# A planner that adds a delay to each result of a recurrent chain, and projections beside it that are given start times

## The chip, the cores and the metric

The kernel runs on one core of a Trainium2 chip. What counts is the device time of one execution in microseconds, here the median of several runs. A core has TensorE (matmul; PE in the profile), VectorE (DVE), ScalarE (ACT), GpSimd (POOL) and SyncE (SP), which here issues most DMAs. Each engine works through its own list of instructions in order and waits for the others by semaphores.

## The reference

Two layers of a backbone over 512 latent and 256 context tokens, width 1024, float32. In each layer a norm, one wide input projection, three token mixers side by side (A: gated linear attention, B: windowed attention, C: RWKV-7 in both directions), a gated merge of their outputs, and a gated feed-forward network. In layer 1 only the latent tokens are needed behind the mixers.

```python
def rwkv7_scan(r, w, k, v, kk, a, s0, with_out):      # mixer C, one direction
    def step(S, inp):
        w_t, k_t, v_t, kk_t, a_t = inp[:5]
        sa = jnp.einsum('bhvk,bhk->bhv', S, kk_t)
        S = S * w_t[:, :, None, :] - sa[..., None] * (kk_t * a_t)[:, :, None, :] + v_t[..., None] * k_t[:, :, None, :]
        ...
        return S, jnp.einsum('bhvk,bhk->bhv', S, inp[5])
    s_fin, y = lax.scan(step, s0, xs)

def merge_branches(ys, gate_logits, w_branch, w_out):
    gates = jnp.split(gate_logits, N_BRANCH, axis=-1)
    m = jax.nn.sigmoid(gates[0]) * (ys[0] @ w_branch[0])
    for i in range(1, N_BRANCH):
        m = m + jax.nn.sigmoid(gates[i]) * (ys[i] @ w_branch[i])
    return m @ w_out
```

## The kernel before

All matrices are cut into tiles of 128 rows. A float32 product is made from three products of a high and a low part (`wh`, `wl`, `hh`, `hl`). A layer runs through the norm, mixers A and B, then the stage that the change touches, then the last branch product, the merge and the feed-forward network.

The touched stage computes mixer C in chunks of 32 tokens. The 768 tokens are six groups of four chunks; a forward and a backward direction (`f`, `b`) go through the groups in opposite orders. Each of these is a stream of operations:

- `loads` and `load_v` bring a group's operands in; `prep` (line 1564) scales them and makes `X`, the products within a chunk.
- `invert` (line 1638) inverts the triangular 32 × 32 blocks of one group of both directions at once. It sends `X` to DRAM (line 1657), reads it back spread out as `L` (line 1660), runs 31 pairs of VectorE instructions (`ftmp`, `G`, lines 1669 and 1670), sends `G` to DRAM (line 1676) and reads it back as the factors `TT` (line 1679). `G` and `L` have one buffer each, so one inversion follows the other.
- `chain` (line 1681) carries the state through the 24 chunks of its direction: `yp` on TensorE, its copy `ysb` on ScalarE, `up` on TensorE with the factors `TT`, copies into `uv` on ScalarE, `sp` on TensorE, and the new state `sblkf` or `sblkb` on VectorE (line 1751). The old state's scaling `scf`, `scb` (line 1719) may run on VectorE, GpSimd or ScalarE.
- `tails` finishes a group's output once both directions have passed it.
- `beside` (line 487) runs work that the chain doesn't need: 24 jobs of 24 products, 16 gate projections and 8 branch products of mixers A and B. In layer 0 each product has a part of 512 and one of 256 columns (`px`, `pz`), in layer 1 only the first. Each job needs its weights loaded (`raw`), split (`wh`, `wl`) and a bank of PSUM; gates leave through ScalarE (line 547), branch products through VectorE (line 576).

The order of all these instructions is made by a planner, `Flow` (line 1866), while the program is built. A stream yields an `Op` with its engine, its cost, what it reads, writes, takes and gives back, and the planner keeps a clock for each engine. It takes the stream whose next operation could start first (its bias is added to that time), books the cost, and notes when the result is there: for TensorE 0.2 us after the end, for a DMA its given latency. A reader on another engine waits 0.12 us more. Only the order of instructions reaches the chip, not the planned times. `chain`, `load_v`, `after` and `summed` (the last two lie in `beside`) have the bias 0, `prep` and `invert` 0.2, the loads of weights 0.2, the products 0.6, the tails 0.4.

Of the kernel before, what the change touches and what calls it, by code (L numbers as in the profile page):

```python
# [19 lines left out]
NX, NZ, NT = 512, 256, 768  # L20
# [8 lines left out]
class Kern:  # L29
    def __init__(self, ctx, tc, I, out, dbg=None):  # L30
        self.ctx, self.tc, self.nc = ctx, tc, tc.nc
        self.I, self.out, self.dbg = I, out, dbg or {}
        self.jobs = deque()
        self.ready = deque()
        self.LOOK = 2
        self.gxb, self.more = 2, None
        self.pin, self.mark = 2, None
        self.hops, self.done = None, 0.0
# [448 lines left out]
    def beside(self, F, l, n, W):  # L487
# [5 lines left out]
        parts = ((0, NX), (NX, n)) if n > NX else ((0, NX),)  # L493
        raws, ws, px, yh, yl, gl = {}, {}, {}, {}, {}, {}
        gw = lambda a, b: 0.232 if b - a == NX else 0.12
        def raw():
            for j, src in enumerate(srcs):
                for e in range(2):
                    yield Op("SP", 0.55, (), ("raw", j, e), take=(("raw", (j, e)),), lat=3.5)
                    raws[j, e] = W.tile([128, 512], F32, name="raw", tag="raw", bufs=3)  # L500
                    nc.sync.dma_start(raws[j, e], src[:, 512 * e:512 * e + 512])
# [22 lines left out]
        def gemms():  # L524
            for j in range(16):
                for a, b in parts:
                    yield Op("PE", 0.0, take=(("gx", (j, 0, a)),))
                    bank(j, 0, a, b)
                for e in range(2):
                    for a, b in parts:  # L530
                        for c in range(4):
                            yield from product(j, 0, a, b, e, c, e == 0, self.h(0, 4 * e + c, a, b), self.h(1, 4 * e + c, a, b))
            yield Op("PE", 0.0, (), "h")
            for j in range(16, 24):
                for o in range(2):
                    for a, b in parts:
                        yield Op("PE", 0.0, (("yab", o),), take=(("gx", (j, o, a)),))
                        bank(j, o, a, b)
                        for c in range(4):
                            yield from product(j, o, a, b, o, c, True, yh[o, c][:, a:b], yl[o, c][:, a:b])  # L540
# [742 lines left out]
class Rwkv:  # L1283
# [354 lines left out]
    def invert(self):  # L1638


        nc, T = self.nc, self.T
        for i in range(6):
            k = lambda name, d="": (name, d, i)
            gs = {d: self.SEQ[d][i] for d in "fb"}
            yield Op("ACT", 0.45, (), k("G"), take=(("G", i),), lat=3.3)
            G = T.tile([128, 2, 8, 32], F32, name="G", tag="G", bufs=1)
            nc.scalar.dma_start(G, self.I["gid"])
            d1, L = {}, None
            for z, d in enumerate("fb"):
# [9 lines left out]
                L = L or T.tile([128, 2, 32, 32], F32, name="L", tag="L", bufs=1)  # L1659
                nc.sync.dma_start(L[:, z].rearrange("u j i -> u (j i)"), d1[d].rearrange("q u j i -> (q u) (j i)").unsqueeze(1).to_broadcast([32, 4, 1024]))  # L1660
            tmp = None
            for n in range(31):
                a, m = n // 4 + 1, 31 - n
                yield Op("DVE", 2 * (0.158 + 0.00105 * 2 * a * m), (k("L", "f"), k("L", "b"), k("G")), k("T"), give=(("L", i),) if n == 30 else ())
                if tmp is None:
                    tmp = T.tile([128, 256], F32, name="ftmp", tag="ftmp", bufs=1)
                t = tmp[:, 0:2 * a * m].rearrange("q (d a b) -> q d a b", d=2, b=m)
                o = G[:, :, 0:a, n + 1:32]
                nc.vector.tensor_tensor(out=t, in0=G[:, :, 0:a, n:n + 1].to_broadcast([128, 2, a, m]), in1=L[:, :, n:n + 1, n + 1:32].to_broadcast([128, 2, a, m]), op=ALU.mult)  # L1669
                nc.vector.tensor_tensor(out=o, in0=o, in1=t, op=ALU.subtract)  # L1670
# [184 lines left out]

class Op:

    def __init__(self, eng, cost=0.0, read=(), write=None, take=(), give=(), lat=None, psum=False):
        self.psum = psum
        self.engs = None if isinstance(eng, str) else eng  # L1860
        if self.engs:
            eng, cost = eng[0]
        self.eng, self.cost, self.read, self.write, self.take, self.give, self.lat = eng, cost, read, write, take, give, lat


class Flow:
# [22 lines left out]

    def begin(self, op):  # L1890

        t = 0.0
        for r in op.read:
            if r not in self.at:
                return None
            at, eng = self.at[r]
            t = max(t, at + (self.HOP if eng != op.eng else 0.0))
        seen = {}
        for tag, _ in op.take:
            bufs, turn, end = self.tags[tag]  # L1900
            i = len(turn) + seen.get(tag, 0) - bufs
            seen[tag] = seen.get(tag, 0) + 1
            if i >= 0:
                if i not in end:
                    return None
                t = max(t, end[i] + self.HOP)
        if op.lat is not None:
            t = max(t, self.dmas[0])
        return t

    def run(self):
        while True:
            heads = []
            for s in list(self.list):
# [12 lines left out]
                if r is not None:  # L1927
                    op = s[2]
                    if op.engs:
                        op.eng, op.cost = min(op.engs, key=lambda e: max(r, self.idle(e[0], op)) + e[1] + self.DEAR.get(e[0], 0.0))  # L1930
                    t = max(r, self.idle(op.eng, op))
# [12 lines left out]
            _, t, s = best  # L1944
# [8 lines left out]
            if op.lat is not None:  # L1953
                self.dmas.append(done)
            if op.write:
                self.at[op.write] = done, op.eng if op.lat is None else "DMA"
            for tag, own in op.take:
                turn = self.tags[tag][1]
# [160 lines left out]
```

## Time and profile before

| what | us |
|---|---|
| median of 3 runs (3235.82 to 3251.81) | 3243.07 |
| the profiled execution | 3247.46 |
| its span, first to last instruction | 3245.6 |
| TensorE busy, share of the span | 2951.2 (91%) |
| VectorE busy | 1760.7 (54%) |
| ScalarE busy | 1202.0 (37%) |
| mixer C's stage, layer 0 | about 650 to 1096 |
| mixer C's stage, layer 1 | about 2345 to 2757 |

The profile holds one execution. Times in it run from the first instruction. A busy TensorE is not one at its peak, since matmuls overlap and their ends are modelled. The granted clock is given as a share of 2.4 GHz: 1.00 is that, 0.50 is 1.2 GHz, and numbers between are means over a stretch.

### The profile page before, as it was taken

What the parts mean: (1) busy time and instruction counts of PE and PEld (TensorE: products, weight loads), DVE (VectorE), ACT (ScalarE), POOL (GpSimd) and SP (SyncE); (2) the same over time, 40 slices, a digit from 0 to 9 for tenths busy, and PEclk for the clock granted to TensorE, in tenths of its full rate; (3) what the DMA queues carried; (4) which work ended last, traced back from release to release, by engine and by line L of the source; (5) the groups of instructions that cost most, each with busy time, mean ns of one, the idle gap of its engine ahead of it and who ended that gap; (6) DMA issues with size and microseconds to landing.
All of it is one profiled execution on the core that took longest, in us unless ns stands there. A gap on an engine that the chain in (4) does not pass through costs nothing. (4 is left out here: it accounts for less than half of the span.)

```text
span 3245.6 us, 62087 instructions
## 1 busy us (share of the span) xinstructions
PE 2951.2 (91%) x25760; PEld 2362.6 (73%) x25760; DVE 1760.7 (54%) x3455; ACT 1202.0 (37%) x2498; POOL 558.7 (17%) x429
## 2 busy tenths in 40 slices
PE   6999999879989889999999899889779887899998
PEld 3777877657767678888888787667556665888887
DVE  3185666766786745222223536646567767653335
ACT  3154454435443333212112434444335444332223
POOL 3033212200001222101001203212200111220102
PEclk9999999889989989999999899989889885899999
DMA  7421322355455542443222322213365652623333
GB/s 292 159 77 59 105 73 106 106 168 157 144 161 163 163 159 91 147 160 134 62 65 79 106 78 82 76 69 104 134 187 162 183 154 62 201 72 98 93 102 117
DMA packets 276282, 398.30 MB, mean 123 GB/s; under 512 B 96928, under 2 KB 178592, under 8 KB 276000
## 3 DMA queue, kind: packets, MB, share of 16 engines
q1 hardware_dynamic: 250528, 360.77, 34.9%
q10 hardware_dynamic: 25472, 33.56, 3.1%
q8 instruction: 202, 3.31, 0.4%
q14 instruction: 80, 0.66, 0.1%
HBM read 320.33 MB, written 73.92 MB: 121 GB/s over the span
## 5 line engine op out<-in xcount | busy, mean ns | idle before, releaser
L50 PE MATMUL px<-hh,wh 128*128 128x512 f32 x1584 | 644.3, 407 | 14.8 <-ACT gat L473 4.6
L50 PE MATMUL px<-hl,wh 128*128 128x512 f32 x1584 | 636.8, 402 | 9.2 <-POOL hl L302 7.9
L50 PE MATMUL px<-hh,wl 128*128 128x512 f32 x1584 | 636.8, 402 | 5.8 <-DVE wl L510 3.1
L71 ACT ACTIVATE wh<-raw 128x1024 fp32r<-128x1024 f32 (+1 forms) x266 | 275.5, 1039 | 722.4 <-PE pz L50 375.6
L72 DVE TENSOR_TENSOR wl<-raw,wh 128x1024 fp32r<-128x1024 f32 (+1 forms) x266 | 333.0, 1253 | 341.5 <-ACT wh L71 311.5
L50 PEld LDWEIGHTS px<-hh,wh 128*128 128x128 f32 x1584 | 304.3, 192 | 105.3 <-issue 25.8
L50 PEld LDWEIGHTS px<-hh,wl 128*128 128x128 f32 x1584 | 304.1, 192 | 81.6 <-issue 8.0
L50 PEld LDWEIGHTS px<-hl,wh 128*128 128x128 f32 x1584 | 304.1, 192 | 77.3 <-POOL hl L302 13.1
L50 PE MATMUL pz<-hh,wl 128*128 128x256 f32 x872 | 250.7, 288 | 1.3 <-DVE wl L72 0.8
L50 PE MATMUL pz<-hh,wh 128*128 128x256 f32 x872 | 249.9, 288 | 2.1 <-DVE fs L729 1.4
L50 PE MATMUL pz<-hl,wh 128*128 128x256 f32 x872 | 250.0, 287 | 1.9 <-DVE hl L304 1.4
L739 POOL TENSOR_TENSOR al<-fs,ah 128x768 fp32r<-128x768 f32 (+1 forms) x44 | 85.0, 1931 | 727.8 <-ACT ah L738 727.8
L50 PE MATMUL px<-y,wh 128*128 128x512 f32 (+1 forms) x512 | 158.8, 395 | 35.1 <-ACT y L123 13.6
L50 PEld LDWEIGHTS pz<-hh,wh 128*128 128x128 f32 x872 | 167.3, 192 | 10.9 <-issue 2.3
L50 PEld LDWEIGHTS pz<-hl,wh 128*128 128x128 f32 x872 | 168.1, 193 | 9.1 <-issue 2.0
L50 PEld LDWEIGHTS pz<-hh,wl 128*128 128x128 f32 x872 | 168.0, 193 | 6.0 <-issue 3.9
L50 PEld LDWEIGHTS px<-y,wh 128*128 128x128 f32 x512 | 96.1, 211 | 58.7 <-ACT y L123 14.3
L1736 ACT COPY uv<-up 32x128 f32<-32x128 f32 x384 | 98.1, 255 | 69.6 <-PE up L1727 57.6
L50 PE MATMUL px<-ah,wh 128*128 128x512 f32 x296 | 116.1, 393 | 0.0
L1670 DVE TENSOR_TENSOR G<-G,ftmp 128x120 f32<-128x120 f32 (+24 forms) x372 | 108.8, 293 | 12.8
L1669 DVE TENSOR_TENSOR ftmp<-G,L 128x120 f32<-128x120 f32 (+24 forms) x372 | 107.3, 288 | 15.4 <-DMA L<-d 5.3
L50 PE MATMUL px<-ah,wl 128*128 128x512 f32 x296 | 115.3, 390 | 0.0
(460 smaller groups left out, 5776.1 us busy)
## 6 DMA issues: line engine op xcount, KB each, us to landing
raw<-w SPq DMA_DIRECT2D x104, 512.0 KB, 3.5
araw<-wada SPq DMA_DIRECT2D x96, 512.0 KB, 5.0
raw<-win SPq DMA_DIRECT2D x82, 512.0 KB, 3.5
raw<-w SPq DMA_DIRECT2D x48, 448.0 KB, 3.4
raw<-win SPq DMA_DIRECT2D x64, 256.0 KB, 3.4
kr<-krd SPq DMA_DIRECT2D x24, 512.0 KB, 4.9
L<-d SPq DMA_DIRECT2D x24, 512.0 KB, 4.5
gs<-gat ACTq DMA_DIRECT2D x24, 384.0 KB, 3.1
```

The source lines that it names most:

```text
L50: return self.nc.tensor.matmul(out, lhsT=lhsT, rhs=rhs, start=start, stop=stop)
L71: nc.scalar.activation(h[:, :n], raw[:, :n], AF.Copy)
L72: nc.vector.tensor_tensor(out=lo[:, :n], in0=raw[:, :n], in1=h[:, :n].bitcast(F32), op=ALU.subtract)
L739: nc.gpsimd.tensor_tensor(out=al, in0=s, in1=ah.bitcast(F32), op=ALU.subtract)
L1669: nc.vector.tensor_tensor(out=t, in0=G[:, :, 0:a, n:n + 1].to_broadcast([128, 2, a, m]), in1=L[:, :, n:n + 1, n + 1:32].to_broadcast([128, ...
L1670: nc.vector.tensor_tensor(out=o, in0=o, in1=t, op=ALU.subtract)
L1736: nc.scalar.copy(uv[ru, p].rearrange("q e v -> q (e v)"), up[32 * p:32 * p + 32, :])
```

## The change

The planner adds 0.6 us to the time at which a result is there, if its stream has the bias 0 and it is not a DMA; buffers that the same operation gives back come free as much later. An operation can be given a time before which the plan doesn't start it (`since`). In layer 1, where a product has one part, job j of `beside` gets 14 j us, and for the branch products the second half 7 us more; in layer 0 nothing is set. The planned cost of a pair of `invert` goes from 2 (0.158 + 0.00105 e) to 2 (0.17 + 0.0012 e), with e elements a row.

```diff
@@ beside
+        pace = 0.0 if n > NX else 14.0
...
-                    yield Op("PE", 0.0, take=(("gx", (j, 0, a)),))
+                    yield Op("PE", 0.0, take=(("gx", (j, 0, a)),), since=pace * j)
...
-                        yield Op("PE", 0.0, (("yab", o),), take=(("gx", (j, o, a)),))
+                        yield Op("PE", 0.0, (("yab", o),), take=(("gx", (j, o, a)),), since=pace * (j + 0.5 * o))
@@ invert
-                yield Op("DVE", 2 * (0.158 + 0.00105 * 2 * a * m), (k("L", "f"), k("L", "b"), k("G")), k("T"), give=(("L", i),) if n == 30 else ())
+                yield Op("DVE", 2 * (0.17 + 0.0012 * 2 * a * m), (k("L", "f"), k("L", "b"), k("G")), k("T"), give=(("L", i),) if n == 30 else ())
@@ Op
-    def __init__(self, eng, cost=0.0, read=(), write=None, take=(), give=(), lat=None, psum=False):
-        self.psum = psum
+    def __init__(self, eng, cost=0.0, read=(), write=None, take=(), give=(), lat=None, psum=False, since=0.0):
+        self.psum, self.since = psum, since
@@ Flow.begin
-        t = 0.0
+        t = op.since
@@ Flow.run
             if op.write:
+                if s[1] == 0.0 and op.eng and op.lat is None:
+                    done += 0.6
                 self.at[op.write] = done, op.eng if op.lat is None else "DMA"
```

## Rows read from the trace of the kernel before

**Rows 1.** Busy time by stretch: start:end, length, engines (instructions), clock, DMA, GB/s

```profile
650.00:1096.00 446.00, 402.17 (x5853) 308.46 (x5852) 319.46 (x777) 190.09 (x545) 42.67 (x34) 0.92 0.52 155
2345.00:2757.00 412.00, 342.20 (x4935) 247.24 (x4930) 292.03 (x719) 178.66 (x513) 44.36 (x35) 0.81 0.51 149
2345.00:2660.00 315.00, 271.10 (x3659) 196.76 (x3654) 230.20 (x544) 142.74 (x387) 35.83 (x28) 0.90 0.59 174
2660.00:2757.00 97.00, 71.10 (x1276) 50.48 (x1276) 61.83 (x175) 35.91 (x126) 8.53 (x7) 0.52 0.27 68
```

**Rows 2.** Same view, instructions of `px` alone: PE, PEld, DVE, ACT, clock, DMA

```profile
2660.00:2685.00 25.00, 0.00 (x0) 0.00 (x0) 0.00 (x0) 0.00 (x0) 0.52 0.49 124
```

**Rows 3.** Costliest groups of the page: count, busy us, mean ns, idle before

```profile
L1670 DVE TENSOR_TENSOR G<-G,ftmp 128x120 f32<-128x120 f32 (+24 forms) x372 | 108.8, 293 | 12.8
L1669 DVE TENSOR_TENSOR ftmp<-G,L 128x120 f32<-128x120 f32 (+24 forms) x372 | 107.3, 288 | 15.4 <-DMA L<-d 5.3
```

**Rows 4.** Stretches of the VectorE phases: layer 1's first, last, sum; layer 0's sum

```profile
2376.90:2401.90 25.00, 10.26 (x93) 8.51 (x92) 23.01 (x72) 4.90 (x9) 1.32 (x1) 0.66 0.31 99
...
2686.70:2708.00 21.30, 12.96 (x224) 9.17 (x224) 18.93 (x70) 7.49 (x28) 0.00 (x0) 0.50 0.06 20
sum 167.90, PE 134.08 PEld 97.12 DVE 147.40 ACT 75.25 POOL 12.49; mean PE 22.35 PEld 16.19 DVE 24.57 ACT 12.54 POOL 2.08
...
sum 200.40, PE 177.88 PEld 136.65 DVE 170.67 ACT 91.52 POOL 20.66; mean PE 29.65 PEld 22.77 DVE 28.45 ACT 15.25 POOL 3.44
```

**Rows 5.** Timeline, VectorE, layer 1: start, length, engine, line, operation

```profile
2401.72 0.19 DVE L1670 TENSOR_TENSOR G<-G,ftmp 128x16 f32<-128x16 f32 x1
```

**Rows 6.** Line 1660 near 2425, the second load of L: issue and landing

```profile
L1660 SPq DMA_DIRECT2D L<-d x1: 519/519/519, 2425.1 to 2425.1; - x1
...
DMA to landing us min/median/max: 5.6/5.6/5.6
```

**Rows 7.** Timeline, VectorE; in brackets the idle time before and its releaser

```profile
2433.39 0.88 DVE L1751 TENSOR_TENSOR sblkb<-sp,scb 64x256 f32<-64x256 f32 x2 [1.20 <-PE sp L50]
2434.30 0.87 DVE L1719 TENSOR_TENSOR scb<-sblkb,pc 64x256 f32<-64x256 f32 x2
2435.20 0.22 DVE L1669 TENSOR_TENSOR ftmp<-G,L 128x62 f32<-128x62 f32 x1
...
2437.59 0.86 DVE L1751 TENSOR_TENSOR sblkf<-sp,scf 64x256 f32<-64x256 f32 x2 [1.40 <-PE sp L50]
```

**Rows 8.** Stretches from L's landing to the next inversion, sums: layer 0, layer 1

```profile
sum 28.00, PE 28.00 PEld 20.52 DVE 15.46 ACT 11.74 POOL 0.25; mean PE 5.60 PEld 4.10 DVE 3.09 ACT 2.35 POOL 0.05
...
sum 21.50, PE 21.50 PEld 14.74 DVE 13.78 ACT 11.63 POOL 4.21; mean PE 4.30 PEld 2.95 DVE 2.76 ACT 2.33 POOL 0.84
```

**Rows 9.** Timeline, VectorE: the longest wait within a phase, layer 0 and layer 1

```profile
828.10 0.86 DVE L1751 TENSOR_TENSOR sblkb<-sp,scb 64x256 f32<-64x256 f32 x2 [4.52 <-PE sp L50]
...
2624.24 0.86 DVE L1751 TENSOR_TENSOR sblkb<-sp,scb 64x256 f32<-64x256 f32 x2 [2.29 <-PE sp L50]
```

**Rows 10.** Timeline, VectorE, layer 1: two successive forward state updates among projections

```profile
2492.65 0.88 DVE L1751 TENSOR_TENSOR sblkf<-sp,scf 64x256 f32<-64x256 f32 x2 [1.46 <-PE sp L50]
...
2500.14 0.86 DVE L1751 TENSOR_TENSOR sblkf<-sp,scf 64x256 f32<-64x256 f32 x2 [1.07 <-PE sp L50]
```

**Rows 11.** Timeline, TensorE, layer 1: two successive `sp`, one of each direction

```profile
2675.22 1.12 PE L50 MATMUL sp<-uv,bkt 64*64 64x64 f32 x16
...
2679.02 1.12 PE L50 MATMUL sp<-uv,bkt 64*64 64x64 f32 x16
```

**Rows 12.** Timeline, VectorE, layer 1's last group: first and fourth backward update

```profile
2729.03 0.88 DVE L1751 TENSOR_TENSOR sblkb<-sp,scb 64x256 f32<-64x256 f32 x2 [1.55 <-PE sp L50]
...
2755.26 0.86 DVE L1751 TENSOR_TENSOR sblkb<-sp,scb 64x256 f32<-64x256 f32 x2
```

**Rows 13.** Timeline, TensorE: the first product behind the stage, layer 0 and layer 1

```profile
1107.88 1.65 PE L50 MATMUL px<-y,wh 128*128 128x512 f32 x3 [6.40 <-ACT y L123]
...
2757.92 0.79 PE L50 MATMUL px<-y,wh 128*128 128x256 f32 x2 [1.98 <-ACT y L123]
```

## The prediction

> **What bounds the kernel now.** I read the two stages first, by the table of stretches [rows 1]. The stage that the change touches takes 446 us in layer 0 and 412 us in layer 1, of a profiled execution of 3247.46 us. TensorE is busy 402 and 342 us of them, so it is not idle long, but in layer 1 the last 97 us are different: the granted clock there is 0.52 (nearly all at the lower level, 1.2 GHz), and the projections are over (no projection matmul in the next 25 us, [rows 2]).
>
> Then I looked for what repeats. Per layer the kernel makes six inversions, one behind the other: 62 VectorE instructions (lines 1669 and 1670), by the page (108.8 + 107.3)/12 = 18.0 us each [rows 3]. In layer 1 the first begins at 2376.9 and the sixth ends at 2708.0 [rows 4], 331 us of the 412. The six VectorE phases add to 167.9 us, so the five intervals between them take 163 us. One such interval, in order of time: the last subtraction of the first inversion starts at 2401.72 [rows 5]; the result goes to DRAM and back, the next block goes out, and the last load of L is issued at 2425.1 and takes 5.6 us, so it lands at 2430.7 [rows 6]. The next inversion starts only at 2435.20. In the 4.5 us between, VectorE executes state updates of the chain which wait for TensorE's `sp` (1.20 us ahead of the one at 2433.39), and the inversion is queued behind them on VectorE [rows 7]. I call this the **hand-over**. All ten add to 28.0 us in layer 0 and 21.5 us in layer 1 [rows 8]. The remaining 163 − 21.5 = 142 us, 28.3 us each, are DMA legs.
>
> So the stage is bounded by a serial loop: DMA legs 28, hand-over 4 to 6, VectorE phase 28 to 33. Inside the phases the same wait occurs again: 12 waits of state updates on `sp` in layer 0, 16.2 us in all, the longest 4.52, and 5 in layer 1, 6.8 us, the longest 2.29 [rows 9]. The chain has slack in each turn of the loop; it ends the stage only after the last inversion.
>
> **The change, part by part.** No instruction is added or removed. All four edits alter the planner's clock, and through it the order on each engine.
>
> Edit 1, +0.6 us on each result of the streams with bias 0. One chain step in the plan (yp, ysb, up, u, sp, S with 0.12 between engines and 0.2 after TensorE) is 0.57 + 0.40 + 0.52 + 1.22 + 0.72 + 1.00 = 4.43 us; with six delays it is 8.03. In a stretch full of projections the trace shows 7.49 us between two updates of one direction [rows 10]. So the plan lags by 3.1 us a step. By the code's latencies the factors TT of the forward direction land 16.8 us before the next L; 16.8/4.43 puts 3.8 steps of the forward chain ahead of the next inversion on VectorE, and, since the backward factors land 5.3 us later, 2.6 of the backward one. Three steps lag 9.3 us; the legs themselves lag 28.8 − 25.4 = 3.4 us behind the plan's; that leaves 5.9 us of waiting, beside a measured mean of 49.5/10 = 4.95. The arithmetic holds, so I use it for after: 16.8/8.03 and 11.5/8.03 put 2.1 and 1.4 steps ahead.
>
> Layer 1: TensorE's own share of two chain steps is 2 × 1.9 us at full clock (3.80 a step near the half clock, [rows 1, 11]). Projections, spread by the pace, fill 5.57/14 = 40% of a slot of 8.03, 3.2 us, and prep and changes of stationary operand about 1; in sum 8.0, no lag. The hand-over falls to between 0 and 1 us. I take −21 of 21.5 and −7 of the waits inside the phases. Against it: about one state update per turn, 0.88 us, with its scaling, 0.87 us [rows 7], moves from the legs, where VectorE has time, into the phase: 5 × 1.75 = +9. Layer 1: −19.
>
> Layer 0: there the projections are half as many again (by the code 576 matmuls of 256 columns more) and unpaced, so the free part of a slot, 8.03 − 2.84 = 5.2 us, is mostly filled: 3.8 + 5.2 + 1 to 2.3 = 10.0 to 11.3 us a step, a lag of 2.0 to 3.3. Two steps lag 4.0 to 6.6 us, less 3.4: a hand-over of 0.6 to 3.2 us instead of 5.6, so −12 to −25; I take −15, near the slower end, since the observed 7.49 was also above its parts. Inside the phases the lag goes on growing over two to three further steps: between −5 and +15; I take +4. The moved update costs +9 again. Layer 0: −2.
>
> Edit 2, the pace in layer 1: job j of 24 not before 14 j us in the plan, the last half at 329. Ahead of that it removes the saturation reckoned above. At the end, projections now run beside the last group. There the chain alone took 8.7 us a step, (2755.26 − 2729.03)/3, at the half clock [rows 12]; at about 8 us: −3, with bounds of −13 (full clock, no projection in the way: the plan's 4.43 and 1 for prep) and +10 (11.3 a step, reckoned above). The weights of the next stage were loaded long before, since the projections' buffers were free by 2660. Now these come free late. Layer 0, where projections run to the end, waits 6.40 us on its first operand behind the stage, layer 1 1.98 [rows 13]; that bounds the cost by 0 and +4.4; I take +2. Edit 3 replaces the plan's cost of one inversion, 16.3 us (sum over line 1664), by 18.0, which is what the page shows [rows 3]; what it does alone is within the bounds above, I put it at 0. Edit 4 (the same +0.6 on gates and branch sums) delays release of a projection bank in the plan; the other bank's twelve or more matmuls cover that, and if not, it is 0.6 us × 24 a layer in the plan only: 0 here, +5 as bound.
>
> A rule to weigh against edit 2: first the rows. With chain work alone TensorE was busy 73% of the last 97 us, and the granted clock was 0.52; in the 315 us before, with projections, it was 0.90 [rows 1]. The Trainium skill (TensorE: Matmul & The Clock Gate, HAM oscillation — how this bites in real kernels) says that bursts of matmuls with idle time between them fall back to the half clock again and again, and that work should be kept together; by that, spreading the projections is the wrong direction. The sum by the rows is the one above; by the rule it is rival 3.
>
> **Sum**: −19 − 2 − 3 + 2 = −22, so 3225.5 us for an execution like the profiled one. That one lies 4.4 us above the median of the three runs (3243.07), so the forecast is 3221, rounded to **3222**.
>
> **Rivals.**
> 1. *The wait only moves.* More projection between two chain steps makes each step longer by as much as the plan now allows, and the updates that no longer hold up the start of an inversion hold up its middle. For it: TensorE is busy 28.00 of the 28.00 us of layer 0's hand-overs [rows 8], so `sp` is late for work, not for order. Against: layer 1 has spare TensorE time over its stage. Then −22 shrinks to about −3: 3240.
> 2. *The whole wait goes.* If layer 0 also loses its hand-overs and phase waits, 13 of its hand-overs and 16 + 4 in its phases are more than I took: 33 us, so 3189 with all of it, 3196 with four fifths. For it: all these waits have the one releaser, `sp` [rows 7, 9].
> 3. *Clock.* In layer 1 TensorE's work per turn at full clock is 8 × 1.9 + 4 × 5.6 + about 8 for prep = 45 us, in a turn of 331/5.5 = 60 us. It becomes the bound when the mean granted clock of the stage falls under 45/60 = 0.75; it is 0.81 now [rows 1]. At 0.69 a turn is 65 us, +5 × 6 = +30, with layer 1's gain gone: 3243 + 30 − 5 = 3268. For it: the 0.52 above. Against: in layer 0 jobs of 5.6 + 2.9 us follow each other about every 446/24 = 19 us, and the clock is 0.92.
> 4. *The stretched last group*, slower. If layer 0's projections still reach into the group after its last inversion, its four steps take 11.3 instead of about 8: +13, and phase waits at their bound another +11, while layer 1 gives −10: 3257. It decides by whether more than two of the 24 jobs are left then.
> 5. *The pace does not spread.* Planned times are not kept on the chip; if the planned stage is shorter than 329 us, the jobs beyond it stand behind the chain, 5.6 us each. With three of them, +17 eats the gain: 3239. My sum of the plan's parts (29 before the first inversion, five turns of 46 to 52, 25 + 10 + 36 at the end) is 330 to 360, so it should just fit.
>
> **How the numbers follow.** Forecast 0.46 (its own range 3208 to 3234), rivals in order 0.14, 0.15, 0.08, 0.10, 0.07. The range 3187 to 3258 leaves out rival 3, half of rival 4 and a third of rival 2, 0.18. A measurement of this kernel can tell about 0.5% from no change, 16 us, so faster is under 3227: 0.37 of the forecast and rival 2, 0.52. Same: the rest of the forecast, rival 1 and most of rival 5, 0.29. Slower, over 3259: rival 3, rival 4 with its edge, and the tail of rival 5, 0.19.
>
> **What would show it.** Right: the ten hand-overs add to 15 to 25 us instead of 49.5; three to four state updates, not six, stand between the factors' landing and the next inversion; projections run past 2700 in layer 1 and the clock of its last 97 us rises above 0.8. Edit 1 wrong: hand-overs shorter and VectorE phases longer by the same. Edit 2 wrong: projections behind the last state update, or the stage's clock under 0.75. The forecast is wrong if layer 1's stage does not shorten by at least 10 us, or if layer 0's grows.

## The result, and the profile after

The changed kernel takes 3275.28 us (median of 5 runs, 3259.58 to 3280.84) beside 3245.69 us for the kernel before on the same chip (5 runs): ratio 1.007, 95% interval 1.0041 to 1.0098 (the two medians alone would give 1.009). The forecast was 3222 us (3187 to 3258), a gain of 0.7%; what came is a loss of 0.7%. The profiled execution, the fastest of the five, took 3259.58 us (span 3257.7), 12.1 us more than that of before.

The table takes the profiled executions apart as the prediction did, in us (L0 and L1 are the layers). A *leg* runs from the last subtraction of an inversion to the landing of the next L, a *hand-over* from there to the next inversion's first instruction, a *phase* over an inversion's VectorE instructions. "Delay" and "pace" are runs of these edits alone, told below. Up to 0.6 us beside the sums of [rows 4] and [rows 8] are where the stretches were cut.

| part | L1 before | L1 after | L1 delay | L1 pace | L0 before | L0 after | L0 delay |
|---|---|---|---|---|---|---|---|
| 5 legs | 141.8 | 139.3 | 135.2 | 142.9 | 133.7 | 166.4 | 153.0 |
| 5 hand-overs | 21.4 | 25.3 | 15.5 | 33.3 | 27.4 | 16.5 | 17.0 |
| 6 phases | 167.9 | 178.1 | 174.4 | 166.8 | 201.0 | 194.5 | 196.5 |
| last phase to the chain's last copy | 47.3 | 45.7 | 46.8 | 46.2 | 53.0 | 47.9 | 52.5 |
| to the first product behind the stage | 2.6 | 2.9 | 2.8 | 2.4 | 10.1 | 3.0 | 3.0 |
| sum | 381.0 | 391.3 | 374.7 | 391.6 | 425.2 | 428.3 | 422.0 |

The 12.1 us are +3.1 and +10.3 in the two stages, 3.9 less ahead of the first, 3.5 less between them, and 6.3 more behind layer 1's stage (494.0 us from its first product to the end, 487.7 before). How far such sums differ by chance can be seen in layer 0: ten profiled executions have the same plan there (before, e2, e5 to e11 and e13), and their sums go from 420.7 to 427.7, their hand-overs from 25.3 to 27.6, their legs from 133.5 to 139.2.

The stages of after by stretch, the same view as [rows 1]: start:end, length, busy us of PE, PEld, DVE, ACT, POOL, then granted clock, DMA share, GB/s.

```profile
650.00:1096.00 446.00, 411.38 (x5782) 316.05 (x5783) 307.55 (x744) 195.46 (x570) 38.14 (x33) 0.90 0.54 156
2345.00:2757.00 412.00, 343.95 (x4832) 246.81 (x4832) 268.81 (x675) 186.26 (x549) 37.77 (x28) 0.80 0.51 148
2345.00:2660.00 315.00, 264.11 (x3548) 191.80 (x3549) 206.41 (x510) 146.06 (x411) 30.52 (x23) 0.81 0.53 153
2660.00:2757.00 97.00, 79.85 (x1285) 55.01 (x1283) 62.40 (x165) 40.20 (x138) 7.26 (x5) 0.77 0.45 128
```

The mean clock of layer 1's stage is what it was, 0.80 beside 0.81. But the last 97 us have risen from 0.52 to 0.77, and the 315 us before have fallen from 0.90 to 0.81. The mean hides that; the intervals between two inversions show it. First before (same view, layer 1), then after:

```profile
2401.91:2435.20 33.29, 28.93 (x420) 19.75 (x418) 19.18 (x35) 15.24 (x46) 1.34 (x1) 0.95 0.66 180
2464.67:2498.59 33.92, 33.92 (x499) 24.18 (x497) 20.31 (x36) 16.94 (x48) 3.88 (x5) 1.00 0.68 185
2525.22:2557.88 32.66, 30.94 (x583) 23.00 (x581) 23.62 (x38) 16.16 (x46) 5.16 (x3) 0.85 0.71 195
2587.54:2621.48 33.94, 32.99 (x515) 23.91 (x514) 21.50 (x33) 15.68 (x46) 10.41 (x8) 0.98 0.64 180
2657.42:2686.74 29.32, 20.84 (x427) 14.40 (x428) 10.74 (x23) 8.15 (x33) 2.31 (x2) 0.56 0.51 136
```

```profile
2398.34:2431.92 33.58, 32.19 (x405) 23.35 (x402) 17.26 (x29) 14.76 (x41) 4.28 (x3) 0.90 0.64 171
2459.01:2489.66 30.65, 23.50 (x349) 17.83 (x347) 16.87 (x25) 12.04 (x34) 2.64 (x3) 0.82 0.67 181
2519.82:2557.32 37.50, 30.55 (x450) 22.45 (x450) 14.43 (x25) 16.38 (x46) 5.06 (x3) 0.77 0.60 160
2584.79:2618.00 33.21, 20.88 (x415) 16.51 (x413) 17.39 (x28) 15.39 (x44) 4.41 (x4) 0.54 0.62 172
2653.33:2682.91 29.58, 27.25 (x294) 19.11 (x293) 13.05 (x22) 10.28 (x30) 1.77 (x1) 0.94 0.79 225
```

Projections lie where the plan was told to put them. In the stretch where before had none [rows 2], `px` alone (PE, PEld, DVE, ACT, clock, DMA) shows in after:

```profile
2660.00:2685.00 25.00, 15.70 (x53) 9.53 (x51) 3.44 (x5) 0.00 (x0) 0.93 0.78 220
```

The first products behind the two stages, as in [rows 13], by the timeline of TensorE:

```profile
1106.98 1.22 PE L50 MATMUL px<-y,wh 128*128 128x512 f32 x2 [4.60 <-ACT y L123]
...
2763.78 0.80 PE L50 MATMUL px<-y,wh 128*128 128x256 f32 x2 [3.23 <-ACT y L123]
```

The sums of the hand-overs (layer 0, layer 1) and of layer 1's phases, as in [rows 8] and [rows 4], then layer 1's sixth phase by itself:

```profile
sum 16.56, PE 16.56 PEld 12.28 DVE 14.23 ACT 8.16 POOL 1.40; mean PE 3.31 PEld 2.46 DVE 2.85 ACT 1.63 POOL 0.28
...
sum 25.28, PE 23.79 PEld 17.06 DVE 14.49 ACT 12.61 POOL 1.85; mean PE 4.76 PEld 3.41 DVE 2.90 ACT 2.52 POOL 0.37
...
sum 178.12, PE 155.51 PEld 106.30 DVE 148.18 ACT 92.83 POOL 10.53; mean PE 25.92 PEld 17.72 DVE 24.70 ACT 15.47 POOL 1.75
...
2682.91:2715.20 32.29, 28.26 (x485) 18.59 (x484) 26.81 (x85) 16.84 (x59) 0.00 (x0) 0.98 0.45 136
```

So the delay did in layer 0's hand-overs what it should (27.4 to 16.5 us), and in layer 1 the hand-overs grew by 4 us and the phases by 10. Of the phases the sixth alone grew by 11, from 21.3 [rows 4] to 32.3 us, of which VectorE was busy 26.8 instead of 18.9: the jobs beside it bring work to VectorE too, the splits of their weights and their sums.

What VectorE didn't work in layer 1's phases and hand-overs, length less busy time, is its waiting: 28.2 us before (20.5 and 7.7), 40.7 after (29.9 and 10.8). Its work there hardly changed (161.2 and 162.7 us), so this waiting is what the loop lost.

### The profile page after: what moved, and what is told of

Its sections match the earlier page's. It is cut to its first block, busy times and chain, and to the rows that moved or that the text cites. A ratio compares the mean times of both kernels' runs of the same rounds, so it can differ in the third digit from the quotient of the medians.

```text
span 3257.7 us, 62093 instructions
## 1 busy us (share of the span) xinstructions
PE 2967.5 (91%) x25760; PEld 2374.0 (73%) x25760; DVE 1735.2 (53%) x3425; ACT 1223.8 (38%) x2578; POOL 544.3 (17%) x419
## 5 line engine op out<-in xcount | busy, mean ns | idle before, releaser
L50 PE MATMUL px<-y,wh 128*128 128x512 f32 (+1 forms) x512 | 157.1, 394 | 32.2 <-ACT y L123 17.0
L50 PEld LDWEIGHTS px<-y,wh 128*128 128x128 f32 x512 | 97.1, 214 | 52.5 <-ACT y L123 17.6
L50 PE MATMUL px<-al,wh 128*128 128x512 f32 x296 | 115.3, 389 | 0.0
```

Of the source, the lines that this page charges most:

```text
L50: return self.nc.tensor.matmul(out, lhsT=lhsT, rhs=rhs, start=start, stop=stop)
```

## The experiments

### Each edit alone

```diff
# e1: delay 0.6, no pace, old cost       # e2: pace 14, no delay, old cost
# e3: new cost of an inversion alone     # e4: after, but buffers come free without the 0.6
```

> The 0.6 us on results alone; the pace and the old cost of an inversion are as before. Theory A (the delay holds back the chain, the chain gives back the operand buffers of layer 0 late, so X of the third and fourth inversion is late): layer 0's legs before the third and fourth inversion stay at 40 us or more (24.4 and 29.0 before), layer 0's loop is about 10 us longer, layer 1 within 5 us of before, the whole +5 to +20 us. Rival B (the loss is all from the pace): within 5 us of the kernel before, legs of layer 0 at 25 to 30 us.

Measured: 3243.82 us, ratio 0.9983 (0.9963 to 1.0004). Hand-overs fell in both layers, by much less than 21 in layer 1. The time is as rival B had it; theory A's legs of 40 us did not come, though two of layer 0 grew to 35.8 and 35.9. VectorE waits 27.0 us in layer 1's phases and hand-overs, nearly what it did before.

> Start times in layer 1 alone, no delay, old cost. Theory A: layer 0 is as before; in layer 1 the projections run beside the last inversion, whose phase grows from 21 to 30 us or more, and the weights of the next stage come late: +8 to +18 us. Rival B: +20 us or more, the whole loss. My prediction would have given -3 to -20.

Measured: 3266.51 us, ratio 1.0063 (1.0041 to 1.0084). The pace alone carries the loss. The sixth phase is 30.9 us, as theory A had it; that the hand-overs would grow, to 33.3 us, neither expected. The sums of layer 1's phases and hand-overs put VectorE's waiting at 25.2 and 17.0, 42.2 us:

```profile
sum 166.83, PE 134.91 PEld 96.01 DVE 141.65 ACT 75.26 POOL 12.77; mean PE 22.48 PEld 16.00 DVE 23.61 ACT 12.54 POOL 2.13
...
sum 33.36, PE 32.79 PEld 22.00 DVE 16.38 ACT 14.53 POOL 0.72; mean PE 6.56 PEld 4.40 DVE 3.28 ACT 2.91 POOL 0.14
```

> The planned cost of an inversion's pairs alone. Theory A and rival B both: within 5 us of before. A third theory, that any change of the plan scatters the time by 10 us and more: off by over 10 us in either direction.

Measured: 3258.54 us, ratio 1.0018 (1.0000 to 1.0037): at the edge of what can be told from nothing. Kernel e7 below, a control, shows the same (1.0019). So a plan that is merely another one can move the time by some 0.2%, and differences of 0.1 to 0.3% say little of a cause; the pace's 0.63% is three times that.

> The changed kernel, but the 0.6 us reach readers only, not the release of buffers that the same operation gives back. Theory A in its narrow form (late planned release by 0.6 us holds the loads back): legs of layer 0 before the third and fourth inversion back to 30 us or less, 10 us faster than the changed kernel. If the chain itself is late (its steps are planned 3.6 us longer), the legs stay at 40 us and the time within 5 us of the changed kernel.

Measured: 3268.19 us, ratio 1.0053 (1.0031 to 1.0076), not to be told from after. Layer 0's legs before the third and fourth inversion are 33.0 and 36.6 us (after 41.3 and 43.7), between the two theories. The later release of buffers in the plan costs nothing that can be measured here. The three edits add up within their intervals: −0.17 + 0.63 + 0.18 = 0.64%, beside 0.70% for all of them.

### Which half of the pace, and what in it

```diff
# e5: gates only                                   # e6: branch products only
-  since=pace * (j + 0.5 * o)                      -  since=pace * j
+  since=0.0                                       +  since=0.0
```

> The kernel before with start times in layer 1 for the 16 gate jobs alone (14 j us); the 8 branch products follow as early as they can, and there is no delay and the old cost. In the run of the pace alone the five hand-overs of layer 1 were 33.3 us instead of 21.4, its first five VectorE phases 135.9 instead of 146.7, and its last turn (fifth leg and sixth phase) 61.1 instead of 46.1. Theory T (the loss of the pace is the last turn, where projections now lie beside the sixth inversion; what the earlier turns lose in hand-overs they win in phases): ratio 0.999 to 1.002, sixth phase 21 to 24 us, hand-overs about 30, earlier phases about 137. Theory H (the loss is in the hand-overs, and the last turn is only where it shows): ratio 1.004 to 1.007, hand-overs 30 or more with the earlier phases not shorter than before.

Measured: 3268.91 us, ratio 1.0058 (1.0040 to 1.0076); hand-overs 38.8 us, sixth phase 34.9.

> The other half: start times for the 8 branch products alone (from 224 us on, 7 us apart in the plan), gates as before. Theory T: this carries the loss of the pace, ratio 1.004 to 1.007, sixth phase 29 to 33 us instead of 21.2, hand-overs of the first four turns as before (17 us), and the last update of the state 10 to 15 us later behind the last softmax product than the 409 us of before. Theory H: ratio 0.999 to 1.002, with the sixth phase longer but the turns before it shorter by as much, since nothing of the branch products lies in them.

Measured: 3259.24 us, ratio 1.0040 (1.0010 to 1.0070); hand-overs 21.7 us, sixth phase 35.0, and the stage as long as before (from mixer B's last softmax product to the chain's last copy 409.6 us, before 409.4). Each half loses, and neither theory holds whole: e5 has theory H's ratio, but shorter phases before the sixth (137.3 us, before 146.7), as T had it; e6 has T's ratio, but a stage as long as before, as H had it. The halves also add to more than the whole (0.58 + 0.40 beside 0.63%). What they do is not the same: e6 leaves the hand-overs alone, e5 lengthens them by 17 us, of which 8 are in the first, where the order is still that of before. Where e6 loses its 0.4% is not shown; its profiled execution, at 3253.41 us, is one of its faster.

Compared instruction by instruction, the order on every engine is the same in e2 and e5 up to layer 1's fifth inversion (but for a few TensorE records that start almost together), beside which the branch products begin to stand elsewhere. Their first two intervals are therefore the same instructions; e2, then e5:

```profile
2403.48:2435.85 32.37, 28.82 (x419) 19.52 (x417) 19.18 (x35) 15.23 (x46) 1.34 (x1) 0.95 0.67 186
2465.33:2503.26 37.93, 35.46 (x481) 25.32 (x479) 19.62 (x34) 15.02 (x44) 2.65 (x3) 0.73 0.51 136
```

```profile
2399.76:2439.63 39.87, 36.60 (x421) 24.11 (x419) 19.18 (x34) 15.48 (x46) 1.35 (x1) 0.74 0.57 151
2469.11:2501.28 32.17, 29.70 (x481) 21.75 (x479) 19.62 (x34) 15.04 (x44) 2.65 (x3) 0.89 0.60 160
```

The first interval takes 32.4 us at a clock of 0.95 and 39.9 at 0.74; the second 37.9 at 0.73 and 32.2 at 0.89. Order and work are equal; the granted clock differs, and with it the length, by 7.5 and 5.8 us. So a part of the difference between two profiled executions is chance, in the first interval above all, whose order is that of before too (33.3 us at 0.95).

What the pace adds to it begins with the second interval. In before TensorE has no pause in it (busy 33.92 of 33.92 us, clock 1.00). In e2 and e5 it waits 1.51 us ahead of the same `sp`, and 1.5 to 2 us behind the start of that `sp` the granted clock falls to its lower level, for 20.5 us in e2 and 6.8 in e5 (first e2, then e5, `sp` by the timeline of TensorE and the stretch at 0.50):

```profile
2476.14 1.18 PE L50 MATMUL sp<-uv,bkt 64*64 64x64 f32 x16 [1.51 <-ACT uv L1737]
2477.60:2498.10 20.50, 20.10 (x232) 13.87 (x228) 5.65 (x11) 6.85 (x24) 1.27 (x1) 0.50 0.46 126
...
2479.96 1.18 PE L50 MATMUL sp<-uv,bkt 64*64 64x64 f32 x16 [1.51 <-ACT uv L1737]
2482.00:2488.80 6.80, 6.40 (x100) 5.01 (x92) 2.57 (x4) 3.48 (x13) 0.00 (x0) 0.50 0.64 167
```

With the denser order, in three executions (before, e6 and e11), the second and third interval had 0.85 to 1.00; with the spread one, in two (e2 and e5), 0.73 to 0.89. The third interval begins with a wait of TensorE of 3.09 us in both spread ones; in before its longest is 1.69. Why the clock stays down so much longer in one of the two is open. In a slow turn (e2, third hand-over, 2557.3 to 2566.8), by the timeline of VectorE and TensorE:

```profile
2558.70 0.88 DVE L1752 TENSOR_TENSOR sblkf<-sp,scf 64x256 f32<-64x256 f32 x2 [3.60 <-PE sp L50]
...
2560.18 0.63 PE L50 MATMUL px<-hh,wl 128*128 128x512 f32 x1
2560.74 0.65 PE L1760 MATMUL op<-uv,X 64*32 64x64 f32 x16
2561.32 0.79 PE L50 MATMUL px<-hh,wh 128*128 128x512 f32 x1
...
2565.26 0.86 DVE L1752 TENSOR_TENSOR sblkb<-sp,scb 64x256 f32<-64x256 f32 x2 [4.80 <-PE sp L50]
```

Two updates wait 8.4 us for `sp`, while TensorE works through projections that show 0.63 to 0.79 us each (0.40 to 0.51 in layer 1 of before, from 2487.5 to 2489.5).

The Trainium skill (TensorE: Matmul & The Clock Gate, HAM oscillation — how this bites in real kernels) tells of a kernel whose short bursts of matmuls, parted by waits, start at the half clock again each time, and advises to arrange the loop so that TensorE stays busy. The trace agrees in part: the clock fell behind a wait of 1.51 us that the spread order has and the dense one has not, but in one execution the spread gates still had 0.89.

### Next to no projections

```diff
+                first = f and c == 0 and i == 0
+                if n > NX or first or last and i == 2:
+                    self.mm(ps[a], ws[j, e][x][c], y, first, last and i == 2)
```

> The kernel before, with the same order of instructions, but in layer 1 only the first and the last matmul of every projection bank are issued, 64 of 576 in all, so the gates and branch sums of layer 1 are not the reference's. Loads, splits, exits and the chain stay. It shows layer 1's loop with a TensorE that has next to no projections in it. Theory N (the hand-over is set by how many chain steps the plan puts ahead of the next inversion, five a turn, and by their own length): hand-overs of layer 1 stay at 18 to 24 us (before 21.4); the phases fall to 21 to 26 us each, some 140 in all instead of 167.9; the turns get shorter by 3 to 8 us each. Theory P, on which my prediction rested (the hand-over is projections that stand ahead of sp): hand-overs under 8 us. The time by theory N is 3200 to 3225, by theory P 3185 to 3205.

Measured: 3242.47 us, ratio 0.9980 (0.9963 to 0.9997). Hand-overs 22.2 us, phases 165.5, legs 136.2.

> The same thinning under the plan with the paced start times (no delay, old cost); again the gates and branch sums of layer 1 are not the reference's. It tells whether the longer hand-overs of the pace (33.3 instead of 21.4 us) come from where its projections lie or from the order of the chain's own steps. Theory of place: without the projections the hand-overs are those of the thinned kernel without pace, within 4 us, and the two times agree within 8 us. Theory of order: hand-overs 8 to 14 us above it, time 8 to 18 us above it.

Measured: 3239.00 us, ratio 0.9963 (0.9944 to 0.9983); hand-overs 20.1 us. Layer 1's stage in e9 by stretch, then the sums of layer 1's phases and hand-overs in e10:

```profile
2345.00:2757.00 412.00, 294.06 (x4478) 208.96 (x4479) 297.99 (x747) 182.35 (x521) 45.01 (x38) 0.52 0.53 155
...
sum 161.39, PE 103.15 PEld 68.09 DVE 140.55 ACT 77.19 POOL 12.54; mean PE 17.19 PEld 11.35 DVE 23.43 ACT 12.86 POOL 2.09
sum 20.06, PE 19.95 PEld 14.29 DVE 13.07 ACT 9.61 POOL 1.14; mean PE 3.99 PEld 2.86 DVE 2.61 ACT 1.92 POOL 0.23
```

Without 512 of its 576 projection matmuls layer 1 has hand-overs of the same sum (as theory N had it), and the clock sinks to 0.52 over the whole stage. One by one they differ (0.0, 1.6, 8.2, 7.4 and 4.9 us; before 4.5, 2.7, 4.1, 5.8 and 4.5), and the phases did not fall to N's 140. The chain at 0.52 of the clock takes about as long as the chain with all projections at 0.81. So the time of both theories was too low: it took TensorE's clock as given. And since the clock fell along with the projections, e9 can't tell what makes a hand-over.

The pair e9 and e10 can tell what the pace costs: with the projections out, the paced order costs nothing (theory of place), and VectorE's waiting is 27.8 us (e9 31.6) where the whole pace had 42.2. The pace therefore loses by its projections, not by the order of the chain's steps. How much of it is the clock at which they run, and how much the projections themselves, this pair doesn't show. One part of the pace stays without them: the sixth phase is 31.8 us in e10 too (e9 21.1), VectorE being busy 26.5 of them with the jobs' splits and sums.

### The clock raised by more work

```diff
+        def filler():
+            while len(F.list) > 1:
+                if held:
+                    yield Op("PE", 0.3)
+                    for _ in range(2 if held else 0):
+                        nc.tensor.matmul(held[0][:, 0:128], lhsT=self.ident, rhs=self.ident, start=True, stop=True, skip_group_check=True)
...
+            F.add(filler(), 1.6)
```

> The pace alone (old cost, no delay), and while a paced job waits for its start time, multiplications of the identity by itself (128 columns each, some 190 in all in layer 1) are issued into its bank, where the job's first product overwrites them; they have the lowest priority in the plan. Nothing else of the pace changes, and TensorE only gets more work. Clock theory (the second to fourth interval of the pace is longer because TensorE's granted clock fell there, 0.73, 0.73 and 0.62 against 1.00, 0.85 and 0.98 before): these three clocks rise to 0.85 or more, the second and third interval fall from 37.9 and 37.6 us to 33 to 35, hand-overs from 33.3 to 20 to 26 us, and the ratio from 1.006 to 0.999 to 1.003 (what the projections beside the sixth inversion cost stays). Place theory (a projection ahead of sp is a delay, whatever the clock): more work ahead of sp, so these intervals stay at 37 or grow, hand-overs 33 or more, ratio 1.006 to 1.012.

Measured: 3279.32 us, ratio 1.0100 (1.0084 to 1.0117). The second to fourth interval of layer 1:

```profile
2461.92:2494.39 32.47, 32.47 (x509) 25.43 (x508) 18.32 (x32) 14.60 (x42) 5.20 (x5) 1.00 0.59 161
2518.12:2551.85 33.73, 33.73 (x597) 27.61 (x596) 19.01 (x29) 14.69 (x43) 3.09 (x2) 1.00 0.50 132
2577.39:2611.97 34.58, 31.16 (x525) 24.42 (x523) 19.43 (x33) 17.20 (x51) 1.36 (x2) 0.76 0.65 184
```

In two turns the clock theory holds: 1.00 and 1.00 instead of 0.73 and 0.73, 32.5 and 33.7 us instead of 37.9 and 37.6, hand-overs 18.5 us instead of 33.3. TensorE has no wait over 0.3 us in these two, where e2 had the 1.51 and 3.09 us. In the third turn the clock rose only from 0.62 to 0.76. From the first inversion to the fourth it takes 173.8 us, e2 187.3, before 180.9. The whole is slower all the same, as the place theory had it: from the fourth inversion on, phases of 25.5, 39.1 and 35.4, intervals of 34.6 and 39.9 (clock 0.76 and 0.69 in the fourth interval and fifth phase) and 51.4 us to the chain's end. VectorE's waiting moved: 5.9 us in the hand-overs instead of 17.0, and 33.7 in the phases instead of 25.2. Filling is no remedy, and why its second half is so long stays open.

> The same filling with the delay of 0.6 us as well: the changed kernel but for the planned cost of an inversion. In the changed kernel the second to fourth interval had clocks of 0.82, 0.77 and 0.54. Clock theory: 0.85 or more, hand-overs of layer 1 under 20 us instead of 25.3, ratio 0.996 to 1.002 instead of 1.007. Place theory: ratio 1.006 to 1.012.

Measured: 3273.32 us, ratio 1.0077 (1.0062 to 1.0091); hand-overs 21.7 us. The third interval fell from 37.5 to 31.4 us with its clock up from 0.77 to 1.00, but the second grew from 30.7 to 34.5 at 0.95. With the delay as well, the ratio is what the place theory had, so the clock alone does not account for the loss.

### Layer 0's long legs

```diff
# e7: two buffers of kr and X in layer 1           # e8: the same, with the delay in layer 1 alone
-  self.n = n = {"f": 2 if self.zout else 3, "b": 3}
+  self.n = n = {"f": 2, "b": 3}
# e15: delay alone, without it for layer 0's forward chain
+  done += 0.0 if self.layer == 0 and s[0].gi_frame.f_locals.get("d") == "f" else 0.6
```

The sum of layer 0's legs rose by 33 us in after and by 19 with the delay alone, more than the executions of one plan differ there. What SyncE waited for (engine, line, releaser: us, times, longest) in layer 0, after and before, then the loads and the work ahead of the second of these legs in after:

```profile
SPq L1658 <- DVE X L1623: 11.3, 2, 11.1
```

```profile
SPq L1657 <- DVE X L1622: 0.5, 1, 0.5
```

```profile
753.09 0.55 SPq L1550 DMA_DIRECT2D kr<-krd  x1
773.86 0.64 SPq L1550 DMA_DIRECT2D kr<-krd  x1
...
783.50 0.65 PE L1728 MATMUL up<-ysb,TT 32*32 32x64 f32 x16 [4.47 <-DMA TT<-d]
...
787.82 2.35 PE L50 MATMUL xp<-kr,bk 64*64 64x64 f32 x64
...
789.45 1.45 DVE L1623 TENSOR_TENSOR X<-xp,rmask 128x512 f32<-128x512 f32 x2 [10.63 <-PE xp L50]
790.93 0.86 SPq L1658 DMA_DIRECT2D d<-X  x2
```

In before the two loads were issued at 743.45 and 756.34 and `d<-X` at 779.98. A load into `kr` needs the chain to have finished an earlier group, and `xp` stands on TensorE behind an `up` that waits for factors. So the inversion that was to have its wait taken away gets its operand 11 us late. Which of the two, the late load or the `up` that waits, holds it back is not told apart.

> The kernel before with two buffers instead of three for the forward direction's kr and X in layer 1, as layer 0 has them; no delay, no start times. It is the control for the next kernel. Both theories: the plan's chain is early enough, legs of layer 1 within 5 us of the 141.8 of before, ratio 0.998 to 1.004.

Measured: 3257.56 us, ratio 1.0019 (1.0000 to 1.0037); legs 136.7 us.

> The same two buffers in layer 1, with the delay of 0.6 us in layer 1 alone; no start times. Theory B (what the delay loses in layer 0 is the return of the forward buffers of kr and X: the chain runs later, so X of a later group is written later, and the transfer that opens the next inversion waits for it): two of the middle legs of layer 1 grow from 28 to 36 to 44 us as they did in layer 0, the sum of legs from 142 to 160 or more, ratio 1.003 to 1.008. Theory C (the long legs of layer 0 come from its denser projections, not from the buffers): legs 130 to 145 as with three buffers and the delay (135.2), ratio 0.996 to 1.001.

Measured: 3246.21 us, ratio 0.9988 (0.9971 to 1.0005); legs 143.1, hand-overs 6.5, phases 177.9 us. Theory B falls for layer 1: two buffers do not make long legs there. Of the 15 us that left the hand-overs 10 are in the phases.

> The delay alone (no pace, old cost), but in layer 0 only on the results of the backward chain, of the gates and of the sums; the forward chain of layer 0, which has two buffers of kr and X, is planned as before. Layer 1 has the whole delay. Theory B (the two long legs of layer 0, 35.8 and 35.9 us with the delay, come from the forward chain giving back its buffers later): legs of layer 0 at 24 to 31 us each, 140 us or less in all instead of 153.0; with hand-overs of 20 to 25 us, the layer's last operation 5 to 12 us earlier against its first inversion, ratio 0.994 to 0.998. Theory C (they come from layer 0's denser projections and the delay as such): legs stay at 148 us or more, ratio 0.997 to 1.001.

Measured: 3242.28 us, ratio 0.9989 (0.9974 to 1.0004). In layer 0 legs of 29.0, 28.0, 36.9, 25.5, 29.1 us, hand-overs 23.8, phases 172.0; from its first inversion to the last copy 405.1 us (before 415.3, delay 419.0). The second and fourth leg, which the delay had made long (35.8 and 35.9), are short again, and the third is long in their place. The sum of the legs, 148.5, and the ratio are as theory C had them; what got shorter is the phases (196.5 with the delay). That the forward chain has a part in the long legs is therefore likely, and not shown. The 10 us don't reach the end: the first tile of the feed-forward network comes 159.9 us behind that copy instead of 155.9 (delay: 144.9).

### Projections beside the last group

```diff
-  since=pace * (j + 0.5 * o)
+  since=322.0 if n == NX and j > 20 else 0.0
```

> The kernel before, with one start time: in layer 1 the last 3 of the 24 jobs (72 matmuls, about 17 us of TensorE) not before 322 us, which is the end of the last inversion in the plan; everything else as early as it can. So no projection lies beside the sixth inversion, and those three lie beside the last group's chain. Theory S (a projection costs the loop where it lies beside an inversion, about 10 us for 65 of them; behind the last inversion the chain leaves room for it, TensorE waited 16.7 us there): fourth leg and fifth phase together 5 to 10 us shorter, the time from the last inversion to the chain's end 44 to 49 us instead of 47.3, ratio 0.996 to 0.999. Theory R (projections beside the last group stretch the chain, as rival 4 had it): that time is 53 to 62 us, ratio 1.001 to 1.004.

Measured: 3271.47 us, ratio 1.0073 (1.0053 to 1.0093).

> The same start time with the delay of 0.6 us, old cost. If both gains add: ratio 0.994 to 0.997, hand-overs of layer 1 about 15 us or less, the last inversion with next to no projection beside it (21 to 26 us). If what is won in the loop is given back behind the stage, as in the run of the delay alone (the chain ended some 5 us earlier against the stage's start, the last branch product came at the same time): ratio 0.998 to 1.001, with the chain's end 8 to 12 us earlier and the first softmaxed feed-forward tile no earlier.

Measured: 3237.51 us, ratio 0.9970 (0.9955 to 0.9984), the lowest ratio of the complete kernels, 0.3% under before, which is hardly more than a new plan by itself can do; its hand-overs are some 17 us, over the 15 expected, and its profiled execution (3248.83) is the slowest of its 12. From the last inversion to the chain's end, before, e11 and e12:

```profile
2708.00:2755.30 47.30, 36.90 (x625) 26.55 (x625) 31.92 (x84) 18.61 (x65) 6.22 (x5) 0.52 0.25 62
```

```profile
2702.80:2757.70 54.90, 43.81 (x684) 29.18 (x685) 36.83 (x92) 21.64 (x72) 6.86 (x6) 0.86 0.34 96
```

```profile
2698.00:2746.80 48.80, 44.23 (x696) 30.49 (x694) 34.41 (x76) 19.72 (x67) 10.02 (x9) 0.95 0.42 119
```

Three jobs stretch the last group by 7.6 us without the delay (theory R) and by 1.5 with it, at 0.86 and 0.95 of the clock. In e11 the fourth leg, hand-over and fifth phase gave 7.5 us (theory S), so the stage is as long as before (409.0 us); the loss is behind it, in the last output tiles (`yc<-tsq`) and their reload. First e11, then before, then the delay alone (e1):

```profile
2796.00 0.52 SPq L1845 DMA_DIRECT2D yc<-tsq  x1
```

```profile
2777.39 0.52 SPq L1844 DMA_DIRECT2D yc<-tsq  x1
2780.51 1.91 SPq L602 DMA_DIRECT2D yraw<-yc  x4
```

```profile
2765.75 0.52 SPq L1845 DMA_DIRECT2D yc<-tsq  x1
2774.13 0.52 SPq L1845 DMA_DIRECT2D yc<-tsq  x1
2779.36 1.91 SPq L603 DMA_DIRECT2D yraw<-yc  x4
```

In e1 the chain's last copy ends at 2745.7, 9.6 us earlier than before; the last store is 3.3 us earlier and the reload 1.2. Both directions end together there, and VectorE does two late tails in turns, the last store 28.4 us behind the chain instead of 22.1. From layer 1's first product behind the stage to the end it is 487.7 us in before, 498.6 in e1, 494.9 in e8 and 497.1 in e12, whose stages had become 6.5, 7.5 and 9.2 us shorter: in these profiled executions what the loop won was given back whole.

## Why the prediction was wrong

**The bound was right, one sentence in it was not.** The serial loop of inversions, and VectorE's queue at its hand-overs, are what the runs show. "The chain has slack in each turn of the loop" is wrong in layer 0: with the delay on the chain's results, two legs of 24 and 29 us became 41 and 44 in after, and two of 24 and 25 became 36 with the delay alone. That it is the chain's lateness that does it is argued from the rows above, not shown.

**Edit 1, layer 1: −21 and −7 of waits, +9, sum −19.** Right in sign and mis-sized. The delay alone gave −5.9 in the hand-overs, −6.6 in the legs and +6.5 in the phases, −6.3 in the sum of the table. The row for it was there: VectorE was busy 13.78 of the 21.50 us [rows 8], so 7.7 us were waiting, of which 4.7 went; the rest is work that has to be done somewhere, and I let 21 go and booked back 9. The plan did what was said of it: 3 to 5 state updates stand between the factors' landing and the next inversion in after, 4 to 5 in before. The "about 1" us for prep and changes of stationary operand in this sum comes from no row.

**Edit 1, layer 0: −2.** The delay alone gave −3.2, within what executions of one plan differ by, and by other terms: hand-overs −10.4 (−15 forecast), phases −4.5 (+13 with the moved updates), legs +19.3 (nothing), the gap behind the stage −7.1 (nothing). That the sum came near is luck.

**Edit 2: −3 and +2, with the saturation removed. This is the step that turned the sign.** The forecast let the pace take projections out of the hand-overs. The pace alone costs +0.63%, some 20 us by the ratio (15.8 between the medians), and VectorE's waiting in layer 1's phases and hand-overs grew from 28.2 to 42.2 us; with the projections left out it was 27.8. In the pace's profile (+10.6 in the table) the second and third interval take +8.9 us, at 0.73 of the clock; the fifth interval and the sixth phase take +15.7, and the third to fifth phase give 9.8 back. The sixth phase grows without the projection matmuls too (e10), so the sum's second gap is VectorE's share of a job: it priced the jobs on TensorE and beside the last four chain steps, not their splits and sums beside the sixth inversion. The tail's term was near: −1.1 alone, −1.6 in after. The first product behind the stage waits no longer than before; the +2 stood for it, and the way from there to the end took 6.3 us more.

**Rival 3 came nearest, at the wrong point.** It let the clock decide at a mean under 0.75 over the stage. The mean stayed at 0.80; single turns of after had 0.77 and 0.54, and those are what the loop passes through, one behind the other. That the spread gates open waits on TensorE which the dense order has not, and that the clock falls behind one, e2 and e5 show, and e13 that it stays at 1.00 where they are filled; why it comes back sooner in one than in the other is open, and by e14 the clock is not the whole loss.

**Rival 1** fits the delay alone by its numbers: hand-overs and legs give, phases take, and little is left; its reason, projections between the steps, is not shown. **Rival 4** is what e11 shows for layer 1, though it was written for layer 0. **Rivals 2 and 5** have nothing for them: waits remain, and no projection stands behind the chain in after. **Edits 3 and 4** were put at 0: +0.18% at the edge of the measurement, and none that shows.

**The signs named beforehand:** projections run past 2700 in layer 1, as forecast; the last 97 us reach 0.77, not 0.8; the ten hand-overs add to 41.8 us, not 15 to 25; shorter hand-overs with phases longer by as much, the sign for edit 1 being wrong, came in layer 1 with the delay alone. The two signs for edit 2 being wrong did not come, though it was: no projection behind the last update, and a stage clock above 0.75. Layer 1's stage did not shorten by 10 us, and layer 0's grew by 3.1, each named as what would make the forecast wrong.

## What to carry to other kernels

From a wait in a queue only the idle part can go: read the busy time inside it first. When work is spread out, read the granted clock turn by turn, not over the stage, and price the work at the places where it goes, beside each serial step, on every engine that has a part in it: here a projection cost VectorE its splits and sums too. Before an execution is compared with another turn by turn, look how far executions of one order differ. Before a gain inside a loop is booked, ask what stands behind the loop's end: here the late tails took it back.

## What was not expected of the hardware

Leaving out 512 of 576 projection matmuls of a stage saved 0.2%, while the granted clock of the stage fell from 0.81 to 0.52. And one sequence of instructions took 33.3, 32.4 and 39.9 us in three kernels, at 0.95, 0.95 and 0.74 of the clock (before, e2 and e5).
